# Two sets of small products of an RWKV-7 chunk solver issued together, one per quadrant of the array

## The chip, the cores and the metric

The kernel runs on one core of a Trainium2 chip. The metric is the device time of one execution in microseconds (us), as the median of several runs. TensorE is called PE here, VectorE DVE, ScalarE ACT, GpSimd POOL, and the queue on which most transfers are issued SP.

## The reference

One layer of a hybrid encoder block on a sequence of 512 positions with 1024 channels, all in float32. What matters here is branch B, the RWKV-7 recurrence with 8 heads of 64 channels:

```python
def step(state, inp):
    r_t, w_t, k_t, v_t, a_t, b_t = inp
    sa = jnp.einsum('bhvk,bhk->bhv', state, a_t)
    state = (state * w_t[:, :, None, :] + sa[..., None] * b_t[:, :, None, :]
             + v_t[..., None] * k_t[:, :, None, :])
    y = jnp.einsum('bhvk,bhk->bhv', state, r_t)
    return state, y
...
h = rmsnorm(x, attn_norm_g)
proj = h @ w_in
...
x = x + mixed @ w_out
...
x = x + (jax.nn.silu(u_gate) * u_val) @ w_ffn_down
```

Beside it stand branch A (stick-breaking attention, 8 heads, blocks of 128 queries), per-channel gates that merge the branches, and a feed-forward part with a depthwise convolution (2816 channels).

## The kernel before, in words

Channels lie on the 128 partitions and the 512 positions on the free axis. Dense products are float32 split into two rounded halves, and three products replace one (`mm1`, lines 131 to 136; the input projections by a loop of their own at line 864).

The first stage mixes three streams of work on PE until about 428 us: `dense_stream` (the columns of `w_in`, line 864, one weight tile after another, 24 products of 128x512 per tile), `att_stream` (attention), and four `rw_stream`, one for each pair of RWKV heads (pairs 0 to 3). Each stream is a generator: it issues a piece of work and yields the time that a planner, `interleave`, is to count for it on PE, and the time after which it may go on. The planner picks the next stream by these numbers alone (the table `LAT` and the constants in the yields), and dense products fill what the others leave. The program's own scheduler then orders each engine's instructions from there.

`rw_stream(p)` cuts the sequence into 8 chunks of 64 positions. For each chunk and head it builds the tile `QA` (products of keys, decays and queries, and the value columns 192 to 255), then inverts a triangular 64x64 matrix. The inverse goes in 32-row halves: the diagonal 32x32 blocks are solved on DVE (lines 531 to 541, buffers `N` and `U`), pass through memory (`su`, `st`, lines 544 to 546) and come back as `U1` (line 550) and `TT` (line 553). Then follow, per pair and in this order:

- `pa` (line 560): 16 products of 32x32, copied by DVE to `U1` (line 564);
- `pl` (line 571): 16 products of 64x64, the "Lak V" term, in two halves of four chunks, copied by ACT to `LV` (line 576);
- `pu` (line 582): 16 products of 32x32 that need `U1`, copied by DVE into the corner of `TT` (line 585);
- `px` (line 591): 16 products of 64x64, "T A", that need `TT`, scaled by DVE into `XA` (line 595);
- the serial chain over chunks (lines 607 to 633), whose first product needs `LV` and `TT`.

With `HROWS`, head 0 holds partitions 0 to 63 and head 1 64 to 127. `pl` reads the other head's partitions, so its two heads lie on one diagonal of the 128x128 array; `px` reads the head's own, so its two lie on the other diagonal. The psum tiles of `rw_stream` and of the small products of `att_stream` come from one pool of three banks (`rbank`).

SP issues, in one queue and in order, the weight loads (`wraw`, line 106), the stores and loads of the solver (lines 519 to 553). The weight tiles have two buffers; a tile is cast by ACT (line 108), and its remainder is made by ACT (line 121) and a POOL transfer (line 122).

Of the kernel before, what the change touches and what calls it, by code (L numbers as in the profile page):

```python
# [8 lines left out]
F32 = mybir.dt.float32  # L9
# [7 lines left out]
P = 128  # L17
# [9 lines left out]
CH = 64  # L27
NC = T // CH
# [24 lines left out]
def hybrid_block(ctx: ExitStack, tc: tile.TileContext, xT, w_in, vecs, decay_up, iclr_up, out_gate_up,  # L53
                 w_branch, w_out, w_up, w_down, out):
    nc = tc.nc
    V, A, G, PE = nc.vector, nc.scalar, nc.gpsimd, nc.tensor
# [127 lines left out]
    TT = cpool.tile([P, NC, CH], F32, name="TT")  # L184
# [15 lines left out]
    with tc.tile_pool(name="p0", bufs=1) as p0, \  # L200
# [76 lines left out]
        for j in range(2):  # L277
            hr = slice(64 * j, 64 * j + 64)
# [4 lines left out]
        for j in range(2):  # L283
            hr, ho = slice(64 * j, 64 * j + 64), slice(64 - 64 * j, 128 - 64 * j)
# [52 lines left out]
    rwp = ph1.enter_context(tc.tile_pool(name="rw", bufs=1, reuse_waits="tile"))  # L337
# [17 lines left out]
    def c3(a):  # L355
        return a.rearrange("p (c t) -> p c t", t=CH)

    def rbank():
        return bank(psr, "pr")

    HROWS = ((slice(0, 64), slice(64, 128)), (slice(64, 128), slice(0, 64)))
# [38 lines left out]
    def rw_stream(p):  # L400
# [7 lines left out]
        for j, bn in ((0, "db"), (1, "ib")):  # L408
            pl = rbank()
            PE.matmul(pl, lup[j][:, p * P : (p + 1) * P], wl2[j], start=True, stop=False)  # L410
            hr = slice(64 * j, 64 * j + 64)
# [54 lines left out]
        for h in range(2):  # L466
            hr = HROWS[h][0]
# [3 lines left out]
        for h in range(2):  # L471
            hr = HROWS[h][0]
# [18 lines left out]
        QAs = []  # L491
        for hf in range(2):
            QA = rwp.tile([P, 4, 2, 256], F32, tag="QA", name="QA", bufs=4)
            QAs.append(QA)
            for c2 in range(2):
                pp = [rbank(), rbank()]
                for j in range(2):
                    for h, (hr, _) in enumerate(HROWS):
                        ch = 4 * hf + 2 * c2 + j
# [3 lines left out]
                for j in range(2):  # L503
                    for h, (hr, _) in enumerate(HROWS):
                        ch = 4 * hf + 2 * c2 + j
                        PE.matmul(pp[h][:, j * P : (j + 1) * P], BK[hr, ch].rearrange("p s t -> p (s t)"),  # L506
                                  ARV[hr, ch, 0 : 2 + h : 1 + h], start=True, stop=True)
                for h in range(2):
                    V.tensor_tensor(QA[:, 2 * c2 : 2 * c2 + 2, h, 64:192],
                                    pp[h][:, 0:256].rearrange("p (j n) -> p j n", j=2),  # L510
                                    maskq[:, None, :].broadcast_to([P, 2, P]), op=ALU.mult)
                for h in range(2):
                    A.copy(QA[:, 2 * c2 : 2 * c2 + 2, h].rearrange("p j (s n) -> p j s n", s=4)[:, :, 0:4:3],
                           pp[h][:, 256:512].rearrange("p (j s n) -> p j s n", j=2, s=2))
# [42 lines left out]
        for ch in range(NC):  # L557
            for h in range(2):
                r0, r1 = slice(64 * h, 64 * h + 32), slice(64 * h + 32, 64 * h + 64)
                PE.matmul(pa[r1, ch * 32 : ch * 32 + 32], QAs[ch // 4][r0, ch % 4, h, 160:192], U1[r0, ch],  # L560
                          start=True, stop=True)
        for h in range(2):
            r1 = slice(64 * h + 32, 64 * h + 64)
            V.tensor_copy(U1[r1].rearrange("p q (k g) -> p q g k", g=4),
                          pa[r1, 0:256].rearrange("p (q g k) -> p q g k", q=NC, g=4))
        yield (430, 0)
        pl = rbank()
        for ch in range(NC):
            for h, (hr, ho) in enumerate(HROWS):
                QA = QAs[ch // 4]  # L570
                PE.matmul(pl[hr, ch * CH : (ch + 1) * CH], QA[ho, ch % 4, h, 128:192], QA[ho, ch % 4, h, 192:256],
                          start=True, stop=True)
            if ch == 3:
                yield (530, 0)
        LV = rwp.tile([P, NC, CH], F32, tag="LV", name="LV")
        A.copy(LV, c3(pl))
        yield (530, LAT["pl"][p])
        pu = rbank()
        for ch in range(NC):
            for h in range(2):  # L580
# [4 lines left out]
            V.tensor_copy(TT[r0, :, 32:64], pu[r0, 0:256].rearrange("p (q n) -> p q n", q=NC))  # L585
        yield (430, LAT["pu"][p])

        px = rbank()
        for ch in range(NC):
            for h, (hr, _) in enumerate(HROWS):  # L590
                PE.matmul(px[hr, ch * CH : (ch + 1) * CH], QAs[ch // 4][hr, ch % 4, h, 192:256], TT[hr, ch],
                          start=True, stop=True)
            if ch == 3:
                yield (530, 0)
        V.tensor_tensor(XA, c3(px), GC.broadcast_to([P, NC, CH]), op=ALU.mult)
        yield (530, LAT["x"][p])

        Rg = ARV[:, :, 0, :]
        G.tensor_tensor(Rg[:, 1:NC], Rg[:, 1:NC], GC[:, 1:NC].broadcast_to([P, NC - 1, CH]), op=ALU.mult)
# [3 lines left out]
        for ch in range(NC):  # L603
            QA, ci = QAs[ch // 4], ch % 4
# [12 lines left out]
            if ch < NC - 1:  # L617
                pS = rbank()
                for h in range(2):
                    PE.matmul(pS[64 * h : 64 * h + 64, 0:64], QA[:, ci, h, 0:64], QA[:, ci, h, 192:256],  # L620
                              start=True, stop=True)
# [8 lines left out]
            for h in range(2):  # L630
                PE.matmul(py[64 * h : 64 * h + 64, 0:64], QA[:, ci, h, 192:256], QA[:, ci, h, 64:128],
                          start=(ch == 0), stop=True, skip_group_check=True)
# [22 lines left out]
        cs = slice(p * P, (p + 1) * P)  # L655
# [160 lines left out]
    def dense_stream():  # L816
# [27 lines left out]
        while cur:  # L844
# [14 lines left out]
            else:  # L859
# [21 lines left out]
               x=(998, 814, 570, 793))  # L881
# [203 lines left out]
```

## Time and profile before

| | |
|---|---|
| median of 3 runs | 904.62 us (903.02 to 905.81) |
| the profiled execution | 903.5 us, of which the profiled span is 901.8 us |
| busy, share of the span | PE 96%, DVE 61%, ACT 57%, POOL 14% |
| TensorE clock granted, mean | 0.985 of full speed |
| transfers | 106.95 MB, mean 119 GB/s |

PE is busy nearly all the time, so time is read from what stands on PE, from the few stretches in which it stands still, and from those in which its clock is at half. A row of the trace gives start, duration, engine, line, operation, output and inputs, with a bracket for idle time just before and for what ended it. Matmuls overlap: how fast they follow each other is read from their starts, not their durations. A float32 product leaves two records, so 16 products are x32.

### The profile page before, as it was taken

The numbers are of one execution on the slowest core, as the hardware profiler recorded it, in microseconds if no ns is written. First come the engines' busy times: TensorE is split into PE (matmuls) and PEld (weight loads), VectorE is DVE, ScalarE is ACT, GpSimd is POOL, SyncE is SP. The second block draws the span as 40 slices with busy tenths as digits, with TensorE's granted clock in tenths as the row PEclk, the third lists the DMA queues.
The fourth block names the chain that finished last, engine by engine and source line by source line (L and its number), as shares of the span: only waits on it lengthen the run. The fifth ranks groups of instructions, "written<-read, shape, count | busy, mean of one in ns | idle before, by whom it ended". The sixth has DMA issues, their size and how long they took to land.

```text
span 901.8 us, 12963 instructions
## 1 busy us (share of the span) xinstructions
PE 864.2 (96%) x4718; PEld 668.9 (74%) x4718; DVE 553.9 (61%) x1115; ACT 513.6 (57%) x909; POOL 129.7 (14%) x200
## 2 busy tenths in 40 slices
PE   5898889999999998899999999999999999999998
PEld 3566656676767776667887878888888888888886
DVE  7566797685785583345565557777777777522222
ACT  7887879866876784778554445444444444321120
POOL 2332433224322431222000000000000000000000
PEclk9798999999999999999999999999999999999999
DMA  7365646756548536843764443333333333243431
GB/s 211 84 140 108 134 93 131 150 119 128 120 89 171 124 87 123 180 101 82 240 190 135 140 117 94 93 94 96 103 104 95 94 94 94 88 129 100 128 100 41
DMA packets 175136, 106.95 MB, mean 119 GB/s; under 512 B 29568, under 2 KB 156672, under 8 KB 175072
## 3 DMA queue, kind: packets, MB, share of 16 engines
q1 hardware_dynamic: 161392, 81.61, 32.6%
q0 software_dynamic: 10656, 19.40, 12.7%
q10 hardware_dynamic: 3024, 5.11, 1.7%
q8 instruction: 37, 0.61, 0.3%
q14 instruction: 27, 0.22, 0.1%
HBM read 78.31 MB, written 8.39 MB: 96 GB/s over the span
## 4 chain that ended last, share of the span: by engine, by line
PE 77%; ACT 6%; DVE 6%; DMA 5%; issue 4%; POOL 1%; SPq 1%; ACTq 0%; POOLq 0%; DVEq 0%
PE pf L136 17%; PE pf L135 17%; PE pf L134 17%; PE pd L864 14%; DMA wraw<-in_w_in 3%; DVE tm L537 1%; ACT wlo L121 1%; DVE U L539 1%; PE pz L747 1%; PE pr L506 1%; PE pr L620 1%; PE pr L607 1%; ACT whi L108 1%; ACT t L69 1%; DMA su<-U 1%
## 5 line engine op out<-in xcount | busy, mean ns | idle before, releaser
L108 ACT CAST whi<-wraw 128x1024 fp32r<-128x1024 f32 (+1 forms) x132 | 130.0, 985 | 180.1 <-PE pf L135 143.3
L124 DVE TENSOR_TENSOR wlo<-wraw,whi 128x512 fp32r<-128x512 f32 (+1 forms) x178 | 114.5, 680 | 82.1 <-ACT whi L108 77.7
L134 PE MATMUL pf<-h2h,whi 128*128 128x512 f32 x352 | 137.3, 390 | 0.0
L135 PE MATMUL pf<-h2l,whi 128*128 128x512 f32 x352 | 136.9, 389 | 0.0
L136 PE MATMUL pf<-h2h,wlo 128*128 128x512 f32 x352 | 136.9, 389 | 0.0
L864 PE MATMUL pd<-hhi,whi 128*128 128x512 f32 x296 | 122.7, 414 | 3.3 <-ACT gs L802 2.6
L864 PE MATMUL pd<-hlo,whi 128*128 128x512 f32 x296 | 121.8, 411 | 0.0
L122 POOL DMA_DIRECT2D wlo<-wraw x74 | 65.3, 918 | 193.1 <-ACT wlo L121 118.0
L864 PE MATMUL pd<-hhi,wlo 128*128 128x512 f32 x296 | 85.2, 409 | 2.0 <-DMA wlo<-wraw 1.9
L135 PEld LDWEIGHTS pf<-h2l,whi 128*128 128x128 f32 x352 | 66.1, 188 | 14.0 <-issue 0.2
L134 PEld LDWEIGHTS pf<-h2h,whi 128*128 128x128 f32 x352 | 66.1, 188 | 13.9 <-issue 0.2
L136 PEld LDWEIGHTS pf<-h2h,wlo 128*128 128x128 f32 x352 | 66.1, 188 | 13.6
L864 PEld LDWEIGHTS pd<-hhi,whi 128*128 128x128 f32 x296 | 57.1, 193 | 16.8 <-ACT gs L802 3.0
L136 PE MATMUL pf<-dh,wlo 128*128 128x512 f32 x176 | 69.3, 394 | 0.0
L134 PE MATMUL pf<-dh,whi 128*128 128x512 f32 x176 | 69.3, 394 | 0.0
L135 PE MATMUL pf<-dl,whi 128*128 128x512 f32 x176 | 69.3, 394 | 0.0
L864 PEld LDWEIGHTS pd<-hhi,wlo 128*128 128x128 f32 x296 | 53.8, 190 | 16.3 <-DMA wlo<-wraw 5.0
L864 PEld LDWEIGHTS pd<-hlo,whi 128*128 128x128 f32 x296 | 57.0, 192 | 12.0 <-issue 0.7
L1024 DVE TENSOR_TENSOR u<-pf,rs 128x512 f32<-128x512 f32 x44 | 30.3, 688 | 38.7 <-PE pf L136 38.6
L128 ACT CAST dh<-cv 128x512 fp32r<-128x512 f32 x22 | 13.7, 621 | 62.0 <-DVE cv L1033 62.0
L121 ACT ACTIVATE wlo<-whi 128x512 fp32r<-128x512 f32 x74 | 45.5, 629 | 2.4 <-ACT QA L615 0.7
L135 PEld LDWEIGHTS pf<-dl,whi 128*128 128x128 f32 x176 | 32.9, 187 | 8.3
(308 smaller groups left out, 1626.5 us busy)
## 6 DMA issues: line engine op xcount, KB each, us to landing
wraw<-in_w_up SPq DMA_DIRECT2D x44, 512.0 KB, 3.8
wraw<-in_w_in SPq DMA_DIRECT2D x41, 512.0 KB, 4.0
wlo<-wraw POOLq DMA_DIRECT2D x74, 256.0 KB, 3.8
wraw<-in_w_down SPq DMA_DIRECT2D x16, 512.0 KB, 4.1
wraw<-in_w_branch SPq DMA_DIRECT2D x16, 256.0 KB, 3.1
wraw<-in_w_out SPq DMA_DIRECT2D x8, 512.0 KB, 4.1
gd<-gs ACTq DMA_DIRECT2D x13, 256.0 KB, 3.6
g<-gd SPq DMA_DIRECT2D x13, 256.0 KB, 2.8
```

The costliest lines, as they stand in the source:

```text
L69: ins = A.activation(o, i, func, **kw)
L108: after(A.copy(hi[:, 0:nk], raw[:, 0:nk]), state["last"])
L121: A.mul(lo[:, 0:n], f(hi[:, k0 : k0 + n]), -1.0)
L122: G.dma_start(lo[:, 0:n], raw[:, k0 : k0 + n], accum_op=ALU.add)
L124: V.tensor_tensor(lo[:, 0:n], raw[:, k0 : k0 + n], f(hi[:, k0 : k0 + n]), op=ALU.subtract)
L128: A.copy(hi, src)
L134: PE.matmul(ps, hi, ah, start=first, stop=False)
L135: PE.matmul(ps, hi, al, start=False, stop=False)
L136: PE.matmul(ps, lo, ah, start=False, stop=last)
L506: PE.matmul(pp[h][:, j * P : (j + 1) * P], BK[hr, ch].rearrange("p s t -> p (s t)"), ARV[hr, ch, 0 : 2 + h : 1 + h], start=True, stop=True)
L864: PE.matmul(ps, w_, a, start=(n == 0), stop=(n == len(todo) - 1))
L1024: V.tensor_tensor(u, ps, rs2, op=ALU.mult)
```

## The change

`pl` is no longer issued between `pa` and `pu`, but after `pu`, chunk by chunk with `px`: for each chunk the four products (two heads of each) go out in a row, and each lies in its own quadrant of the array. Both psum banks are taken at once. The planner now counts 650 + 650 for the joint block where it counted 530 four times, and what was the delay after `pl` is the delay between `pa` and `pu`. The copy to `LV` comes after the joint block.

```diff
-        yield (430, 0)
-        pl = rbank()
-        for ch in range(NC):
-            for h, (hr, ho) in enumerate(HROWS):
-                QA = QAs[ch // 4]
-                PE.matmul(pl[hr, ch * CH : (ch + 1) * CH], QA[ho, ch % 4, h, 128:192], QA[ho, ch % 4, h, 192:256],
-                          start=True, stop=True)
-            if ch == 3:
-                yield (530, 0)
-        LV = rwp.tile([P, NC, CH], F32, tag="LV", name="LV")
-        A.copy(LV, c3(pl))
-        yield (530, LAT["pl"][p])
+        yield (430, LAT["pl"][p])
         pu = rbank()
...
         yield (430, LAT["pu"][p])
 
-        px = rbank()
+
+        pl, px = rbank(), rbank()
         for ch in range(NC):
-            for h, (hr, _) in enumerate(HROWS):
-                PE.matmul(px[hr, ch * CH : (ch + 1) * CH], QAs[ch // 4][hr, ch % 4, h, 192:256], TT[hr, ch],
-                          start=True, stop=True)
+            QA, cs = QAs[ch // 4][:, ch % 4], slice(ch * CH, (ch + 1) * CH)
+            for h, (hr, ho) in enumerate(HROWS):
+                PE.matmul(pl[hr, cs], QA[ho, h, 128:192], QA[ho, h, 192:256], start=True, stop=True)
+                PE.matmul(px[hr, cs], QA[hr, h, 192:256], TT[hr, ch], start=True, stop=True)
             if ch == 3:
-                yield (530, 0)
+                yield (650, 0)
+        LV = rwp.tile([P, NC, CH], F32, tag="LV", name="LV")
+        A.copy(LV, c3(pl))
         V.tensor_tensor(XA, c3(px), GC.broadcast_to([P, NC, CH]), op=ALU.mult)
-        yield (530, LAT["x"][p])
+        yield (650, LAT["x"][p])
```

Since the planner's numbers changed, it places other work differently too, from pair 0 on. In the changed program `pu` is line 571, `pl` line 582, `px` line 583, the `LV` copy line 587, and later lines stand 7 lower (dense products line 857, masks and values 737 to 757).

**Pair 1 on PE and ACT.** `pr` are the pool's three banks, `pz` and `po` those of attention. PE before, from `pa` on:

```order
L560 MATMUL pr<-U_95,QA 32x32 x16
L864 MATMUL pd<-hhi,whi 128x512
L864 MATMUL pd<-hlo,whi 128x512
L864 MATMUL pd<-hhi,whi 128x512
L571 MATMUL pr<-QA 64x64 x8
L714 MATMUL pz<-q_1714,k_1830 128x384
L715 MATMUL pz<-q_1714,klo_91 128x384
L716 LDWEIGHTS idb
L716 MATMUL pz<-mskb,idb 128x128
L571 MATMUL pr<-QA 64x64 x8
```

PE in the changed program, at the start of the joint block:

```order
L737 MATMUL pz<-ach,none 128x256
L737 MATMUL pz<-acl,none 128x256
L740 MATMUL pz<-sph_2294,ntri 128x384
L740 MATMUL pz<-spl_2295,ntri 128x384
L756 MATMUL po<-wth,vt 128x256
L757 MATMUL po<-wtl,vt 128x256
L582 MATMUL pr<-QA 64x64
L583 MATMUL pr<-TT,QA 64x64
L582 MATMUL pr<-QA 64x64
L583 MATMUL pr<-TT,QA 64x64
```

ACT before, around the copy to `LV`:

```order
L121 ACTIVATE wlo<-whi 128x512
L69 ACTIVATE e<-pz 128x384
L576 COPY LV<-pr 128x512
L69 ACTIVATE e<-e 128x384
L69 ACTIVATE wth<-pz 128x256
```

ACT in the changed program:

```order
L69 ACTIVATE e<-pz 128x512
L69 ACTIVATE e<-e 128x512
L69 ACTIVATE wth<-pz 128x384
L69 ACTIVATE e<-e 128x512
L69 ACTIVATE w<-pz 128x384
L128 CAST sph_2557<-e 128x512
L587 COPY LV<-pr 128x512
```

The two sets of products alternate one by one, 16 times, in pairs 1 to 3 (in pair 3 two products of attention stand between the halves). In pair 0 the scheduler issues 15 of `pl` in a row, then 15 of `px`, then the last of each. The `LV` copy of pair 1 moved behind the six ACT steps of a 512-wide score tile.

**Pair 1 on SP**, from the solver's store to the loads of the next stage. Before:

```order
L546 DMA st<-N 512x1x8 x4
L553 DMA TT<-su 32x8x32 x3
L519 DMA sc<-QA 32x4x32 x4
L550 DMA U_95<-st 32x8x32 x2
L553 DMA TT<-su 32x8x32
L106 DMA wraw<-in_w_in 128x8x128
```

In the changed program:

```order
L546 DMA st<-N 512x1x8 x4
L553 DMA TT<-su 32x8x32 x3
L550 DMA U_95<-st 32x8x32 x2
L553 DMA TT<-su 32x8x32
L106 DMA wraw<-in_w_in 128x8x128
L519 DMA sc<-QA 32x4x32 x8
```

The loads of `U1` no longer stand behind four stores of pair 2's `QA`.

**Pair 3 on SP**, the same place. Before:

```order
L546 DMA st<-N 512x1x8 x4
L106 DMA wraw<-in_w_in 128x8x128
L553 DMA TT<-su 32x8x32
L550 DMA U_95<-st 32x8x32
L553 DMA TT<-su 32x8x32
```

In the changed program:

```order
L546 DMA st<-N 512x1x8 x4
L553 DMA TT<-su 32x8x32 x3
L550 DMA U_95<-st 32x8x32
L106 DMA wraw<-in_w_in 128x8x128
L550 DMA U_95<-st 32x8x32
```

A weight load of the dense stream now stands behind the first load of `U1`, which waits for the solver's stores to land.

## Rows read from the trace of the kernel before

**Rows 1.** The page: busy time and share of each engine, and the clock by slices.

```profile
PE 864.2 (96%) x4718; PEld 668.9 (74%) x4718; DVE 553.9 (61%) x1115; ACT 513.6 (57%) x909; POOL 129.7 (14%) x200
...
PEclk9798999999999999999999999999999999999999
```

**Rows 2.** Waits of PE from 58 to 430 us: us in total, times, longest.

```profile
PE pd L864 <- ACT gs L802: 2.6, 1, 2.6
```

**Rows 3.** Timeline of PE, pair 0: start, duration, engine, line, operands, shapes.

```profile
156.65 1.15 PE L571 MATMUL pr<-QA 64*64 64x64 f32 x32
157.73 0.69 PE L582 MATMUL pr<-TT,U 32*32 32x32 f32 x32
...
159.71 1.15 PE L591 MATMUL pr<-TT,QA 64*64 64x64 f32 x32
```

**Rows 4.** Timeline of PE, two places where two tiles of the array are used.

```profile
144.38 0.23 PE L501 MATMUL pr<-ident,ARV 64*128 64x64 f32 x2
144.45 0.23 PE L501 MATMUL pr<-ident,BK 64*128 64x64 f32 x2
...
167.83 0.34 PE L620 MATMUL pr<-QA 128*64 128x64 f32 x4
168.00 0.29 PE L631 MATMUL pr<-QA 128*64 128x64 f32 x4
```

**Rows 5.** Timeline of PE, pair 1: the start of `pa`.

```profile
218.54 0.21 PE L560 MATMUL pr<-U,QA 32*32 32x32 f32 x2 [1.81 <-DMA U<-st]
219.06 0.62 PE L560 MATMUL pr<-U,QA 32*32 32x32 f32 x27 [0.31 <-DMA U<-st]
```

**Rows 6.** Timeline of SP's queue, pair 1.

```profile
214.61 1.87 SPq L519 DMA_DIRECT2D sc<-QA  x4
216.53 0.92 SPq L550 DMA_DIRECT2D U<-st  x2
```

**Rows 7.** Chain that ended last, pair 1: start, us, what.

```profile
220.84 1.05 PE pr L571 x16
...
229.12 1.38 PE pd L864 x6
230.50 0.61 PE pr L591 x16
```

**Rows 8.** Windows view: length; PE, PEld, DVE, ACT, POOL busy; PEclk; DMA share; GB/s.

```profile
220.00:224.00 4.00, 4.00 (x39) 2.81 (x38) 2.13 (x5) 0.52 (x2) 1.89 (x4) 0.57 0.76 206
```

**Rows 9.** Timelines of PE, ACT and DVE, pair 1, and the `LV` copy's line.

```profile
228.01 0.23 PE L716 MATMUL pz<-mskb,idb 128*128 128x128 bf16 x1
...
228.28 0.60 ACT L69 ACTIVATE e<-pz 128x512 f32<-128x512 f32 x1 [0.92 <-PE pz L716]
...
231.65 0.63 ACT L128 CAST sph<-e 128x512 fp32r<-128x512 f32 x1
...
230.47 0.69 DVE L721 SCALAR_TENSOR_TENSOR e<-pz,e 128x512 f32<-128x512 f32 x1 [1.59 <-ACT e L69]
...
L576 ACT COPY LV<-pr x4: 581/586/587, 157.8 to 376.5; 128x512 f32<-128x512 f32 x4
```

**Rows 10.** Timeline of SP's queue, pair 3.

```profile
345.40 9.23 SPq L546 DMA_DIRECT2D st<-N  x4
354.80 0.50 SPq L106 DMA_DIRECT2D wraw<-in_w_in  x1
...
357.28 0.33 SPq L550 DMA_DIRECT2D U<-st  x1
```

**Rows 11.** Timeline of DVE, pair 3.

```profile
370.34 1.26 DVE L564 COPY U<-pr 32x256 f32<-32x256 f32 x2 [2.63 <-PE pr L560]
376.16 0.69 DVE L674 TENSOR_TENSOR wtl<-sq,wth 128x512 fp32r<-128x512 f32 x1 [4.55 <-ACT sq L69]
376.77 0.75 DVE L680 SCALAR_TENSOR_TENSOR rawq<-rawq,qg,sq 128x512 f32<-128x512 f32 x1
...
379.63 0.87 DVE L585 COPY TT<-pr 32x256 f32<-32x256 f32 x2
```

## The prediction

> **What bounds the kernel now.** I read the page first. PE is busy for 864.2 of 901.8 us, 96%, DVE for 61% and ACT for 57% [rows 1]: TensorE's queue sets the time, and only three things can change it: work on PE, stretches in which PE stands still, and its clock. The slices of the clock show digits below 9 near the start and, later, hardly at all [rows 1]. The change touches the first stage alone, until about 428 us; the rest is dense products that follow unchanged, so a microsecond that PE gains there arrives at the end. Next I read the waits of PE in that stage and the timelines around the four places where `pa`, `pl`, `pu`, `px` stand. PE waits twice for the loads of `U1` at pair 1's `pa`, 1.81 and 0.31 us [rows 5], and once 2.6 us for the evacuation of a dense bank, late in the stage [rows 2]. Outside those, the moved products run without a gap.
>
> **The joint block.** Sixteen products of `pl` hold PE from 156.65 to 157.73, 1.08 us, and sixteen of `px` start a row of the same length [rows 3]. Both already run two heads at a time. What the trace lacks is four 64x64 tiles at once. Its parts are there. Two row halves that share all columns: each row of two transposes follows the last after 0.07 us though it lasts 0.23, so two go out every 0.07 [rows 4]. Two column halves that share all 128 rows: four records of line 620 are followed by the next group after 0.17 us [rows 4], which one at a time, at the 0.07 of the transposes, would need 0.28. Bounds: if four run at once, the joint block costs 1.08 in place of 2.16 us, a gain of 1.08 per pair; if two, the gain is 0. A loss I exclude, since the block issues the same products in the same tile size. I take 1.08, because each half of the mechanism is seen. In pair 0 the products don't alternate, and I count nothing. For pair 3 see below. Pairs 1 and 2: **-2.2 us**.
>
> A rule speaks against this. The Trainium skill, "TensorE: Matmul & The Clock Gate", Part 3 on row and column tiling, says that a weight load overlaps running matmuls only when its row group differs. `pl` of one head and `px` of the other share their row group, so by that rule only two would run at once and the term would be 0. The rows of line 620 [rows 4] speak against it, but for two tiles, not four. It is a rival below.
>
> **Pair 1's wait.** The loads of `U1` were issued at 216.53, behind four stores (line 519) that held SP's queue from 214.61 for 1.87 us [rows 6]. In the new order they stand ahead of those stores, so they go out about 1.9 us sooner. `pa` also comes later on PE: the new order has 8 more dense products between pair 0's `pa` and pair 1's, at 1.38 / 6 = 0.23 us each [rows 7] 1.8 us, and 8 transposes fewer, at 0.07 [rows 4] 0.6 us. 1.9 + 1.8 - 0.6 is more than the 1.81 + 0.31 = 2.12 us of the wait [rows 5]. The bounds are 0 and -2.1; I take **-2.1 us**. Those dense products are only moved: they are missing later, where something else must cover.
>
> **The clock behind that wait.** After it, half of `pl` took 1.05 us, where half of `px` at full clock took 0.61 [rows 7]. From 220 to 224 us the granted clock averaged 0.57 [rows 8], which is mostly the lower of its two levels, 1.2 GHz against 2.4. PE had stood still before it fell. At full clock the same work needs 4.0 x 0.57 = 2.3 us, so 1.7 is lost. Without the wait there is nothing to lower the clock there; another wait could do so elsewhere. Bounds 0 and -1.7; I take **-1.7 us**.
>
> **Cover that goes.** (a) `pl` stood between `pa` and `pu` while DVE copied `U1`, two copies in 1.26 us [rows 11]. In the new order pair 0 still has its 9 dense products and 8 transposes there, pair 1 has 8 transposes and nine wide products, pair 2 six dense products (1.4 us) and 8 transposes, pair 3 nine (2.1 us): 0. (b) `pl` ran long before `px`, so `LV` was ready early. Now the copy starts after the joint block, and the chain's first product waits for it. In pair 1 the copy stands behind the ACT steps of a 512-wide score. Before, that score ended at 228.24 [rows 9]; DVE's step of it ended at 231.16, the cast `sph` could follow at 231.2 without the weight cast that stood ahead of it, for 0.63 us, and the copy takes 0.59 [rows 9]: 232.4, that is 4.2 us after the score. PE has in that time six mask and value products (0.9 us, an estimate from six of them at 0.15), the joint block (1.1), three dense products (0.7), a small score and tile changes (0.5): 3.2. The chain waits **+1.0 us**; bounds 0 (the copy comes in time) and 2. In pair 2 it stands behind four casts of the keys, and no row times that line; between 0 and pair 1's 1.0 I take **+0.5 us**. In pairs 0 and 3 four or six full-width dense products stand between block and chain, about 0.9 to 1.4 us against 0.6 for the copy: 0.
>
> **Pair 3.** `px` needs DVE's copies into `TT`. In the new order DVE does them behind a split (`wtl`, at 376.16) and the scaling of `q` (376.77 to 377.52) [rows 11], which wait for ACT and not for PE. With the copies' 0.87 us `px` can't start before 378.4; before, the copies ended at 380.5 [rows 11]. PE has three dense products fewer between `pa` and `px`, and no `pl`, so it arrives early and waits there. The saving of this pair is spent on that wait: **0**, between -1.1 (arriving in time) and +1.
>
> **Pair 3's weight load.** Before, it was issued at 354.80, right behind the solver's stores, and the first `U1` load at 357.28, once the stores had landed [rows 10]. Now it stands behind that load: it starts at 357.7 or so unless the solver is done sooner. This tile was already the one PE waited for, 2.6 us [rows 2]. Bounds 0 and +2.9; the solver's last DVE step now stands ahead of three other steps that shared its end, which brings the stores forward, so I take the lower third, **+1.0 us**.
>
> **Sum:** -2.2 - 2.1 - 1.7 + 1.0 + 0.5 + 0 + 1.0 = -3.5 us against the profiled execution's 903.5, so 900.0. The median, 904.62, lies 1.1 above that execution: **901.1 us**. A measurement of this kernel can tell about 0.3%, 2.7 us, from no change.
>
> **Rivals.**
>
> 1. *Two at a time.* The four quadrants don't run at once (the rule above, or the queue not looking far enough ahead). The rest stays: -3.5 + 2.2 = -1.3, 903.3 us. For: no row shows four. Against: both halves of it [rows 4].
> 2. *The weight tile starves PE (slower).* Pair 3's load waits for the solver's stores. If the solver ends 3 us later than before against the dense stream, the load starts at 360.7, 5.9 us later than 354.80 [rows 10], PE stands still that much longer, and the clock falls behind it (+1.7, as in rows 8). -3.5 - 1.0 + 5.9 + 1.7 = +3.1, 907.7 us. It decides from a load that starts some 2.8 us late with the fall of the clock, 4.5 without. For: the load's new place and the wait it already causes [rows 2]. Against: the U1 loads get out of the way of the next tile.
> 3. *The time isn't on the path.* Each pair's chain meets the same landings, casts and copies as before, PE only waits for them elsewhere: 904.6 us. For: pair 3 shows just that. Against: the waits of PE in the middle of the stage are few.
> 4. *Nothing new waits.* -2.2 - 1.1 - 2.1 - 1.7 = -7.1, 897.5 us. Against: the new places of the `LV` copy.
>
> **How the numbers follow.** Forecast 0.42, with a range of its own of 899 to 903; rival 1 0.15; rival 2 0.15; rival 3 0.18; rival 4 0.10. Faster by over 0.3% (below 901.9): nearly all of the forecast (0.38), rival 4, a little of rival 1 (0.02): 0.50. Slower by over 0.3% (above 907.3): 0.13 of rival 2 and 0.04 of rival 3: 0.17. Within: 0.33. The range goes from rival 4's 897.5 to 907.0, which leaves out most of rival 2 and little else.
>
> **What would show it.** In the profile after: records of the joint block in pairs 1 to 3 in groups of four starts and some 1.1 us for all 32 products (right), or 2.1 (rival 1); `pa` of pair 1 without a wait for `U1`, and the clock at 1.00 from 215 to 230 us; the chain's first product waiting for `LV` by about a microsecond in pair 1; the wait for the dense bank after 355 us at 2.6 to 5.5 us. The prediction is wrong if PE's idle time in the stage grows by more than the block saves, above all if the clock falls behind a new wait.

## The result, and the profile after

The changed kernel took 909.46 us (median of 17 runs, 904.49 to 913.80), the kernel before 904.06 in the same comparison: a ratio of 1.0052 (95% interval 1.0035 to 1.0068). It is 0.5% slower, where 901.1 us was forecast and 907.0 was the range's upper end. The profiled execution took 909.66 us (span 908.0, mean granted clock 0.979), 6.2 us more than that of before.

The page of the changed kernel, the same lines as [rows 1]:

```profile
PE 866.8 (95%) x4718; PEld 669.4 (74%) x4718; DVE 554.2 (61%) x1115; ACT 513.5 (57%) x909; POOL 133.1 (15%) x200
...
PEclk9799999999998899999999999999999999999999
```

The work of each engine is what it was. New is the clock: the slices from 272 to 318 us show an 8 where they showed a 9. PE's waits from 58 to 430 us, the view of [rows 2] (us in total, times, longest):

```profile
PE pr L501 <- ACT QA L513: 5.4, 3, 3.1
...
PE pd L857 <- DMA wlo<-wraw: 3.6, 4, 1.3
PE pr L583 <- DVE TT L574: 2.8, 1, 2.8
...
PE pr L600 <- ACT LV L587: 1.0, 1, 1.0
```

The wait for `U1` in pair 1 [rows 5] is gone from the head of the list. The longest is now 3.1 us at line 501, a place whose waits the prediction never mentions: the first products that build `QA` for the next pair. Pair 1 first, PE's timeline from `pa` to the end of the joint block:

```profile
216.53 0.69 PE L560 MATMUL pr<-U,QA 32*32 32x32 f32 x32
...
223.30 0.27 PE L582 MATMUL pr<-QA 64*64 64x64 f32 x1
223.30 0.27 PE L583 MATMUL pr<-TT,QA 64*64 64x64 f32 x1
223.31 0.27 PE L582 MATMUL pr<-QA 64*64 64x64 f32 x1
223.32 0.27 PE L583 MATMUL pr<-TT,QA 64*64 64x64 f32 x1
223.41 0.22 PE L582 MATMUL pr<-QA 64*64 64x64 f32 x1
...
224.39 0.50 PE L857 MATMUL pd<-hlo,whi 128*128 128x512 f32 x1
...
226.72 0.33 PE L600 MATMUL pr<-LV,TT 64*64 64x64 f32 x4 [1.03 <-ACT LV L587]
```

`pa` runs in one piece with no wait. Four products, one per quadrant, start within 20 ns, and all 32 products hold PE from 223.30 to 224.39, 1.09 us, as long as 16 of them before [rows 3]. The clock is at 1.00 from 220 to 224. Then the chain waits 1.03 us for `LV`. So far the sizes are as forecast. Now the place of the 3.1 us, first PE's timeline:

```profile
280.62 0.28 PE L501 MATMUL pr<-ident,BK 64*128 64x64 f32 x2
...
283.30 0.96 PE L857 MATMUL pd<-hhi,wlo 128*128 128x512 f32 x3
287.36 0.36 PE L501 MATMUL pr<-ident,BK 64*128 64x64 f32 x1 [3.10 <-ACT QA L513]
```

And ACT's at the same time:

```profile
281.34 1.26 ACT L679 CAST q<-rawq 64x512 fp32r<-64x512 f32 x2 [0.82 <-DVE rawq L673]
285.99 1.04 ACT L108 CAST whi<-wraw 128x1024 fp32r<-128x1024 f32 x1 [3.40 <-DMA wraw<-in_w_in]
286.94 0.64 ACT L513 COPY QA<-pr 128x256 f32<-128x256 f32 x2
```

PE needs a bank of `rbank`'s three. ACT would free it with the copy of line 513, whose input is ready (in the run below that takes the cast away, the same copies start at 284.02), but on ACT a weight cast stands ahead of the copy, and the cast waits 3.40 us for its load. Behind the wait, the windows of the changed kernel (columns as in [rows 8]):

```profile
284.00:288.00 4.00, 0.90 (x7) 0.64 (x6) 0.51 (x2) 2.01 (x4) 0.00 (x0) 0.79 0.74 188
288.00:292.00 4.00, 4.00 (x54) 3.49 (x53) 2.30 (x5) 0.75 (x3) 0.96 (x2) 0.50 0.46 75
292.00:296.00 4.00, 4.00 (x40) 2.90 (x39) 0.97 (x4) 1.76 (x4) 2.19 (x5) 0.50 0.00 0
296.00:300.00 4.00, 4.00 (x20) 3.01 (x21) 2.11 (x5) 1.89 (x4) 1.03 (x2) 0.50 0.41 71
300.00:304.00 4.00, 4.00 (x71) 2.96 (x70) 2.65 (x6) 2.75 (x6) 2.53 (x5) 0.58 0.61 146
304.00:308.00 4.00, 4.00 (x32) 2.96 (x31) 1.77 (x5) 2.73 (x7) 0.10 (x1) 1.00 0.43 131
```

The clock goes to the lower level and stays there until about 303. From 284 to 304 its mean is 0.57, where before it was 1.00: 20 x 0.43 = 8.6 us. About 0.5 us of that lie in the wait itself, while PE stood still, so some 8 are lost behind it. With the wait that is 11 us, more than the change could have saved.

In the kernel before the same cast stood directly ahead of the same copies in ACT's queue. Its timeline of ACT at that place:

```profile
290.49 1.05 ACT L108 CAST whi<-wraw 128x1024 fp32r<-128x1024 f32 x1 [0.30 <-PE pd L864]
291.44 0.64 ACT L513 COPY QA<-pr 128x256 f32<-128x256 f32 x2
```

And where PE begins to build pair 3:

```profile
284.77 0.69 PE L560 MATMUL pr<-U,QA 32*32 32x32 f32 x32
285.39 0.68 PE L571 MATMUL pr<-QA 64*64 64x64 f32 x16
...
286.80 0.68 PE L571 MATMUL pr<-QA 64*64 64x64 f32 x16
...
288.30 0.27 PE L501 MATMUL pr<-ident,BK 64*128 64x64 f32 x1
```

There the build of pair 3 began at 288.30, and the cast waited for PE (0.30 us) and not for its load. In the changed kernel the build begins at 280.62, 7.7 us sooner, but the cast only 4.5 us sooner (285.99 for 290.49). Pair 1's chain is done 5.3 us sooner (its last copy to `Y` starts at 259.9, before at 265.2). The other 2.4 us come from PE's order around the build: before, `pa` and `pl` of pair 2 stood ahead of it (the rows above); in the changed kernel `pl` is gone from there and `pa` comes at 288.94, behind the stall. PE gained time in both ways and ran into a weight tile that had not gained as much.

### The profile page after: what moved, and what is told of

It reads as the page before. It is cut to its first block, busy times and chain, and to the rows that moved or that the text cites. A ratio compares the mean times of both kernels' runs of the same rounds, so it can differ in the third digit from the quotient of the medians.

```text
span 908.0 us, 12964 instructions
## 1 busy us (share of the span) xinstructions
PE 866.8 (95%) x4718; PEld 669.4 (74%) x4718; DVE 554.2 (61%) x1115; ACT 513.5 (57%) x909; POOL 133.1 (15%) x200
## 4 chain that ended last, share of the span: by engine, by line
PE 75%; DVE 8%; ACT 6%; DMA 5%; issue 4%; SPq 1%; POOL 0%; ACTq 0%; POOLq 0%; DVEq 0%
PE pf L136 17%; PE pf L134 17%; PE pf L135 17%; PE pd L857 13%; DMA wraw<-in_w_in 4%; DVE tm L537 2%; DVE U L539 2%; ACT wlo L121 1%; PE pr L613 1%; PE pz L740 1%; ACT whi L108 1%; PE pr L600 1%; SPq L546 1%; PE pr L506 1%; ACT t L69 1%
## 5 line engine op out<-in xcount | busy, mean ns | idle before, releaser
L134 PEld LDWEIGHTS pf<-dh,whi 128*128 128x128 f32 x176 | 32.9, 187 | 8.2
```

What stands on the lines that cost most here:

```text
L134: PE.matmul(ps, hi, ah, start=first, stop=False)
```

## The experiments

"Build" is the longest wait of PE at line 501 for pair 3, "clock" the mean from 284 to 304 us, both of each run's profiled execution. Where a star stands, the wait ends with another step of ACT (`sq`), which also frees a bank. Ratios are against the kernel before on the same chip.

| kernel | median, us | ratio (95%) | build, us | clock |
|---|---|---|---|---|
| changed, again | 910.33 | 1.0059 (1.0037 to 1.0080) | 3.5 | 0.57 |
| U twice | 910.27 | 1.0064 (1.0042 to 1.0086) | 3.9 | 0.83 |
| block apart | 909.20 | 1.0045 (1.0028 to 1.0061) | 2.0* | 0.74 |
| cast on POOL | 907.81 | 1.0029 (1.0015 to 1.0044) | 2.8 | 0.66 |
| solver first | 911.93 | 1.0066 (1.0046 to 1.0085) | 3.2* | 0.66 |
| both | 912.03 | 1.0075 (1.0060 to 1.0089) | 3.5* | 0.74 |
| planner 1060 | 910.15 | 1.0058 (1.0039 to 1.0077) | 2.8* | 0.50 |
| tile on POOL | 898.74 | 0.9938 (0.9915 to 0.9962) | none | 1.00 |
| tile on POOL, apart | 910.92 | 1.0041 (1.0018 to 1.0065) | 1.9* | 0.52 |
| three raw buffers | 893.97 | 0.9879 (0.9858 to 0.9900) | none | 1.00 |
| three raw buffers, again | 893.04 | 0.9865 (0.9846 to 0.9883) | none | 1.00 |
| three raw buffers, apart | 894.58 | 0.9881 (0.9863 to 0.9899) | 1.0 | 0.67 |
| before, U twice | 903.75 | 0.9979 (0.9966 to 0.9992) | 0.2 | 1.00 |
| before, tile on POOL | 903.63 | 0.9987 (0.9973 to 1.0001) | 0.4 | 1.00 |
| before, three raw buffers | 893.34 | 0.9871 (0.9849 to 0.9893) | none | 1.00 |
| before, three raw buffers, again | 892.79 | 0.9865 (0.9850 to 0.9880) | none | 1.00 |

**One execution?** The changed kernel, profiled once more.

> The changed kernel itself, profiled once more and timed. Its first profile shows PE standing still for 3.10 us at 284.26 (for ACT's copies of QA, which stand behind a weight cast) and the clock at the lower level from 286.33 to 303.39. Theory 'held queue' (a memset that waits for the solver's store holds the weight stream back, so PE stalls and the clock falls): the stall is in the order of the program, so it shows again, between 2.5 and 3.7 us, and the clock falls behind it; 907 to 912 us. Rival 'bad draw' (that profile was one unlucky execution): the stall or the low stretch is missing, and the time is 904 to 907.

The wait is there again, 3.49 us, and the clock is 0.57. It belongs to the order, not to one execution (the fastest of the 17 timed executions, 904.49 us at a mean clock of 0.990, may have lost less; it has no trace).

**What makes the load late.** It went out at 279.81; the two transfers of remainders that free its buffer had left POOL at 274.56, behind a memset of `U` that waits for the solver's store.

```diff
-    U = rwp.tile([P, 8, 32], F32, name="U")
+    U_two = [rwp.tile([P, 8, 32], F32, name=f"U{i}") for i in range(2)]
...
-        G.memset(U, 0.0)
+        U = U_two[p % 2]; G.memset(U, 0.0)
```

> The changed kernel with two buffers for U, so that POOL's memset of the next pair's U does not wait for the store of this pair's. PE's and ACT's orders stay as they are. Theory 'held queue': the two weight remainders that left POOL at 274.56 go out by about 271 and 273, the load at 279.81 starts about 2.5 us sooner, the wait of 3.10 us shrinks below 0.8, and the clock doesn't fall there, which returns 2.5 + 8 us: 898 to 902 us. Rival 'short of cover' (with pl gone from between pa and pu the dense stream runs ahead of its loads, whatever POOL does): the wait stays above 2 us and the time at 907 to 911.

The first transfer went out right behind ACT's step (275.59, with ACT's done at 275.29; in the changed kernel 274.56 and 270.83), so the memset had held them. (This profile runs late throughout: the cast of the tile before stands at 279.81 in place of 275.24.) The wait stayed, 3.9 us: the load now stood on SP behind the solver's stores and loads and went out at 286.43. One link was removed and another, on SP, took over, so the memset alone is not the cause.

The same edit on the kernel before:

> The kernel before with two buffers for U: the control for the run above. In its trace two remainders of the same pair stand behind the same memset too (268.34 and 269.99), but PE shows only 0.42 us of waiting near them. Theory 'held queue': the wait is covered there, so within 0.3% of the kernel before, 902 to 906. Rival 'U alone' (the second buffer is a gain by itself, with or without the joint block): faster by as much as in the changed kernel, 895 to 899.

A ratio of 0.9979: about 2 us, with nothing at the build to remove.

**The block itself.** Taken apart in the same place:

```diff
-        for ch in range(NC):
+        for half, s in ((0, 0), (0, 1), (1, 0), (1, 1)):
+            for ch in range(4 * half, 4 * half + 4):
...
-                PE.matmul(pl[hr, cs], QA[ho, h, 128:192], QA[ho, h, 192:256], start=True, stop=True)
-                PE.matmul(px[hr, cs], QA[hr, h, 192:256], TT[hr, ch], start=True, stop=True)
+                for hr, ho in HROWS:
+                    PE.matmul((pl, px)[s][hr, cs], QA[(ho, hr)[s], HROWS.index((hr, ho)), (128, 192)[s] : (192, 256)[s]],
+                              QA[ho, HROWS.index((hr, ho)), 192:256] if s == 0 else TT[hr, ch], start=True, stop=True)
...
```

> The changed kernel with the joint block taken apart: eight products of pl, then eight of px, twice, in the same place and with the planner's numbers unchanged. No four quadrants at once: the block takes 2.2 to 2.6 us in place of 1.16 in pair 1. The program's scheduler also moves one weight load on SP, pair 2's, from ahead of four solver stores to behind them. Theory 'held queue': what slows the changed kernel isn't the block, so it is slower than the changed kernel by what the quadrants save, 1 to 3 us, or by more where that load lands later still: 910 to 915. Rival 'the block itself' (four at once disturb what follows): faster than the changed kernel, 903 to 907.

As slow as the joined one (1.0045 against 1.0059, intervals that overlap). The edit undoes only part of the concurrency: the block took 1.56 us in pair 1, not the 2.2 to 2.6 expected, and PE still waits 2.0 us at the build. So nothing speaks for four at once as what costs, but this run by itself doesn't exclude it; the run with the tile on POOL, below, does.

**The solver, and ACT.** In the changed kernel the solver of pair 2 ends at 268.9 in place of 262.3, since its last steps alternate on DVE with pair 3's preparation. That could be why PE is left with dense products alone. A rival: the late cast on ACT is enough. The first edit moves that one cast to POOL (it is the 27th of the dense stream); nothing else changes place:

```diff
-        after(A.copy(hi[:, 0:nk], raw[:, 0:nk]), state["last"])
+        state["n"] = state.get("n", -1) + 1; (G.tensor_copy if state["n"] == 26 else lambda o, i: after(A.copy(o, i), state["last"]))(hi[:, 0:nk], raw[:, 0:nk])
```

> The changed kernel with one weight cast, the one that ACT did at 285.99 ahead of four copies of QA, moved to POOL; nothing else changes place on any engine. Theory 'blocked ACT' (PE's 3.10 us at 284.26 come from the copies of QA that stand on ACT behind a cast whose load is late): the copies run at about 284.6, the wait shrinks below 1 us, and the stretch of low clock behind it goes or gets short: 909.8 - 2.5 - (4 to 8) = 899 to 903 us. Rival 'tile late anyway' (PE has drawn the dense stream so far ahead that without this tile it has nothing to do): PE does the build and the 32-row products a little sooner and then stands still at the next dense product for as long, the clock falls all the same, 908 to 911 us.

ACT's timeline with the cast on POOL:

```profile
284.02 0.70 ACT L513 COPY QA<-pr 128x256 f32<-128x256 f32 x2 [1.29 <-DVE QA L509]
287.90 0.63 ACT L121 ACTIVATE wlo<-whi 128x512 fp32r<-128x512 f32 x1 [3.18 <-POOL whi L108]
288.44 0.63 ACT L513 COPY QA<-pr 128x256 f32<-128x256 f32 x2
```

And PE's:

```profile
285.34 0.69 PE L560 MATMUL pr<-U,QA 32*32 32x32 f32 x32
288.85 0.36 PE L501 MATMUL pr<-ident,BK 64*128 64x64 f32 x1 [2.82 <-ACT QA L513]
```

Two copies now run at 284.02, and PE goes on to `pa`. Then ACT stands again, for the remainder of the same tile, with the next two copies behind it. The block moved by one step. The ratio is 1.0029 where the changed kernel had 1.0052 and 1.0059, with intervals that overlap, so it is open how much came back.

The second edit puts pair 3's preparation and pair 1's last steps behind the solver's last step by order-only dependences on DVE (`behind` adds one; two of the four places are shown):

```diff
-        V.tensor_copy(ut, U.rearrange("p k t -> p t k"))
+        state["sol", p] = V.tensor_copy(ut, U.rearrange("p k t -> p t k"))
...
-        V.scalar_tensor_tensor(kk, k, vcol("keyk", p), kk, op0=ALU.mult, op1=ALU.mult)
+        behind(V.scalar_tensor_tensor(kk, k, vcol("keyk", p), kk, op0=ALU.mult, op1=ALU.mult), p == 3)
...
```

> The changed kernel with pair 3's preparation on DVE (from the scaling of kk on, and two projections) and pair 1's last steps put behind the last step of pair 2's solver, with which they alternate in the changed kernel from 258 to 268.5; PE's order stays. Theory 'late solver' (this alternation makes the solver end at 268.9 where it ended at 262.3 before; meanwhile PE runs through its dense products and out of weights): the solver ends by 263, pa of pair 2 starts 3 to 6 us sooner than 288.9, no wait of PE over 1 us from 275 to 295, no stretch of low clock there: 898 to 903 us. Rival 'tile late anyway': the weight loads, which move on SP too, are late still, a wait of 2 us or more and a low clock stay: 907 to 911 us.

The timeline of DVE, the solver's last step:

```profile
262.80 0.41 DVE L541 COPY N<-U 128x256 f32<-128x256 f32 x1
```

ACT's timeline:

```profile
281.57 1.05 ACT L108 CAST whi<-wraw 128x1024 fp32r<-128x1024 f32 x1 [3.89 <-DMA wraw<-in_w_in]
```

PE's waits from 275 to 300 us:

```profile
PE pr L501 <- ACT sq L69: 3.2, 1, 3.2
```

The solver ends at 263.2 (262.3 in the kernel before), and nothing is gained. The solver's transfers now stand ahead of the weight loads on SP, the cast of the tile before the late one waits 3.89 us on ACT, and what stands behind it is a step of the attention (`sq`) that holds another of the three banks. So an early solver is not enough. Whether the late one has a part in the stall stays open, since the edit made another tile late.

> Both edits together: the cast on POOL and the solver first. 'Late solver' and 'blocked ACT' name two links of one chain, so together they return no more than the better of the two, 898 to 903 us. If they are separate costs, the sum of both gains. Under 'tile late anyway' 907 to 911.

No gain either, for the same reason: the tile that is late is now the one before, and its cast is still on ACT (3.80 us of waiting, at 280.95).

**The tile off ACT altogether.** Cast and both remainders of the 27th tile on POOL:

```diff
+        (G.tensor_copy if state["n"] == 26 else lambda o, i: after(A.copy(o, i), state["last"]))(hi[:, 0:nk], raw[:, 0:nk])
...
+        if state.get("n") == 26:
+            G.tensor_tensor(lo[:, 0:n], raw[:, k0 : k0 + n], f(hi[:, k0 : k0 + n]), op=ALU.subtract)
+        elif state.get("dma"):
```

> The changed kernel with all the work on one weight tile, the late one (its cast, and both remainders), on POOL, so that ACT does nothing for it. With the cast alone on POOL, the wait of 3.10 us came 1.7 us later (2.82 us at 286.03), since the next two copies of QA still stood on ACT behind the first remainder of the same tile. Theory 'blocked ACT': now no copy of QA stands behind that tile, PE goes through pair 3's build and meets the tile at its next dense product, by then cast: waits of PE from 280 to 295 under 1 us together, no stretch of low clock or a short one, 900 to 904 us. Rival 'tile late anyway': the wait of about 3 us moves on to the dense product of that tile, and the clock falls: 907 to 910 us.

The timeline of ACT:

```profile
284.07 1.03 ACT L513 COPY QA<-pr 128x256 f32<-128x256 f32 x3 [1.29 <-DVE QA L509]
```

POOL's:

```profile
286.65 1.04 POOL L107 CAST whi<-wraw 128x1024 fp32r<-128x1024 f32 x1 [7.42 <-DMA wraw<-in_w_in]
```

PE's:

```profile
285.39 0.69 PE L560 MATMUL pr<-U,QA 32*32 32x32 f32 x32
286.01 0.27 PE L501 MATMUL pr<-ident,BK 64*128 64x64 f32 x1
```

And the window from 284 to 304 us:

```profile
284.00:304.00 20.00, 19.10 (x244) 13.76 (x244) 12.63 (x29) 13.25 (x33) 9.13 (x13) 1.00 0.41 102
```

The tile is as late as ever (its cast starts at 286.65, where it was 285.99), but only POOL waits for it. PE goes through the build, and when it comes to the tile's products the tile is there. No wait, clock 1.00, and some 10 us less than the changed kernel (0.9938 against 1.0052; the medians, from two comparisons, differ by 10.7). The joint block is in place here, so it is not what costs. This shows the cause: not the late tile alone, but ACT's queue behind the tile.

The control is the same edit on the kernel before:

> The kernel before with the same weight tile's work moved from ACT to POOL; nothing else changes place. The control for the run on the changed kernel that went to 898.7 us. There the tile's load was late against PE; before, its cast at 290.49 has no wait for a load behind it and PE waits 0.42 us near it. Theory 'blocked ACT' (the edit repairs a stall that only the changed order has): within 2 us of the kernel before, 903 to 907, so that the changed kernel with the edit is 0.5 to 0.8% faster than this one. Rival 'a gain of its own' (work taken off ACT helps either way): 897 to 901 us.

0.9987: the edit alone gives nothing that can be told from no change. So it repairs what the change broke, and the change without that stall is worth 0.9938 / 0.9987 = 0.995, some 4.4 us (an estimate across two comparisons).

**The planner's numbers.**

```diff
-                yield (650, 0)
+                yield (1060, 0)
...
-        yield (650, LAT["x"][p])
+        yield (1060, LAT["x"][p])
```

> The changed kernel with the planner counting 1060 + 1060 for the joint block, as much as it counted for pl and px before (4 x 530), in place of 650 + 650. Theory 'planner' (what slows the changed kernel is that the planner, counting 820 less for each pair, places dense work and pair 3's preparation otherwise): the order comes close to the one before, the wait at pair 3's build is under 1 us, 898 to 903 us. Rival 'the move' (pl behind pu is enough to upset pair 2, whatever is counted): a wait of 2 us or more and a low clock there, 907 to 911 us.

The wait (2.8 us) and the low clock (0.50) are there, with a cast at 279.93 that waits 4.95 us on ACT. Counting as much as before doesn't take the stall away: the build still begins ahead of pair 2's `pa` (281.19 and 287.46). That `pl` behind `pu` decides it is the likelier reading, but the order differs from that of before in more than this.

**A third raw buffer.** One of three places that allocate the tile; the other two get the same:

```diff
-        raw = wpool.tile([P, KT, P], F32, tag="wraw", name="wraw")
+        raw = wpool.tile([P, KT, P], F32, tag="wraw", name="wraw", bufs=3)
```

> The changed kernel with three buffers for the raw weight tile in place of two, so that a load needn't wait until both remainders of the tile before last are done (the load at 279.81 went out when the transfer issued at 275.37 had landed). The scheduler moves some other work with it. Theory 'two buffers' (the weight stream can't run further ahead than two tiles, so PE, which now has nothing but dense products from 260 to 281, outruns it): the loads that were at 269.8 and 279.8 go out 3 to 8 us sooner, no wait over 1 us at pair 3's build, no stretch of low clock there: 897 to 903 us. Rival 'blocked queues' (it is the order on SP and ACT, not the buffers): the load stands behind the solver's transfers on SP all the same, 907 to 911.

> The kernel before with three raw buffers, the control for the run above. Theory 'two buffers': before, PE meets no late tile in pair 2, and gains at most its 2.58 us of waiting at 358.86 and a little more: 900 to 904 us. If the third buffer is a gain of its own, 5 us or more here too, 896 to 900.

Both are faster than the kernel before by some 12 us, more than any theory said, and equal to each other. Most of it is waiting, and not at the build alone: by the pages PE stands still for 901.8 - 864.2 = 37.6 us in the kernel before, which waits only 0.42 us at the build, and for 891.4 - 863.1 = 28.3 us in the same kernel with three buffers. No weight cast on ACT waits for a load any more from 262 to 296 us. These are the fastest versions of the study. Timed again together:

> The changed kernel with three raw weight buffers, timed once more beside the two runs below. Theory 'freed' (with the weight stream repaired the change gives what its block saves, 3.3 us less what waits take its place): 1 to 3 us faster than the kernel before with three buffers. Rival 'nothing left' (what the change repairs in pair 1, the wait for U1 and the clock behind it, the third buffer repairs too, and the block's gain goes into the waits for LV, for the remainders and for the bank): within 1 us of it, as the first runs showed (893.97 and 893.34).

> The kernel before with three raw weight buffers, once more, as the other half of that comparison: 892 to 895 us by both.

893.04 and 892.79, both at 0.9865 (0.9846 to 0.9883 and 0.9850 to 0.9880). With the weight stream repaired the change is worth nothing that shows. Its block does run four at a time (1.16 us in pairs 1 and 2 from the first start to the last end), but PE waits for other things. PE's waits from 140 to 430 us, first of the changed kernel with three buffers:

```profile
PE pr L560 <- DMA U<-st: 2.5, 2, 2.3
PE pd L857 <- DMA wlo<-wraw: 2.1, 2, 1.3
PE pr L600 <- ACT LV L587: 1.0, 1, 1.0
PE pr L692 <- ACT QA L513: 0.9, 1, 0.9
```

Then of the kernel before with three buffers:

```profile
PE pr L560 <- DMA U<-st: 2.5, 1, 2.5
PE pd L864 <- ACT rawq L374: 1.1, 1, 1.1
```

With the joint block PE waits 1.0 us for `LV`, 0.9 for a bank and 2.1 for remainders, without it 1.1 for a dense bank, and pair 1's wait for `U1`, the largest thing the change removed, is gone in both but for 0.2 us (the 2.3 and 2.5 us of line 560 are pair 0's). In the two profiles PE is busy 861.2 us with the joint block and 863.1 without, and stands still 29.8 us and 28.3. So most of what the block saves is waited away; these are single executions, and that the waits listed are the whole reason is argued, not shown.

**Four quadrants alone.** Two attempts to price them by taking the block apart where nothing stalls:

> The changed kernel with that tile on POOL and with the joint block taken apart (eight products of pl, then eight of px, twice, in the same place). Against the 898.7 us with the block joined it shows what the four quadrants give once no stall covers it. Theory 'quadrants': 1.08 us in each of pairs 1 to 3, less where the block is waited for anyway: 901 to 903 us. Rival 'hidden': 898 to 900. The scheduler moves one load on SP as it did with the first kernel of this kind, so a wait of over 1 us at pair 3's build in its trace would make it undecided.

Undecided by its own condition: it waits 1.9 us at the build, behind the cast of another tile (4.79 us on ACT), and its clock is 0.52. Two of its twelve executions took 903.12 and 903.90 us, at mean clocks of 0.988 and 0.985; the other ten took 907.4 to 912.9, at 0.974 to 0.981.

> The changed kernel with three raw buffers and the joint block taken apart, eight products of pl, then eight of px, twice, in the same place. With two buffers this comparison was undecided, since a late tile stopped PE. If PE has no wait over 1 us for a late tile from 260 to 300 us, it shows what four quadrants at once give. Theory 'quadrants': 1.08 us in each of pairs 1 to 3, 2 to 4 us slower than with the block joined. Rival 'hidden': within 1 us of it.

894.58 against 893.04 us, ratios 0.9881 (0.9863 to 0.9899) and 0.9865: slower by 1.5 us with intervals that overlap, so not settled. In pair 1 the block took 1.57 us from its first start to its last end, not 2.2: eight of one set run into eight of the other, so taking it apart that way undoes only part of the concurrency. And the 1.5 us can't be put down to the block: PE waits 1.24 us for `U1` in pair 1 and 0.99 at the build, and its clock falls behind that wait (profiled was the slowest of the five executions, 896.95 us). With the block joined PE waits 0.2 us for `U1`, not at all at the build, and the clock is 1.00. PE's timeline with the block apart, and the windows behind it:

```profile
282.31 0.27 PE L501 MATMUL pr<-ident,BK 64*128 64x64 f32 x1 [0.99 <-ACT QA L513]
```

```profile
282.00:290.00 8.00, 7.69 (x95) 6.18 (x96) 3.30 (x8) 3.46 (x9) 3.19 (x6) 0.60 0.66 148
290.00:298.00 8.00, 8.00 (x89) 6.02 (x89) 4.56 (x9) 4.64 (x9) 3.56 (x6) 0.54 0.52 110
```

## Why the prediction was wrong

**Joint block, -2.2: right in size.** 32 products in 1.09 us in pair 1; in pair 2 they fell into the low clock (301.92 to 303.66, 1.74 us) and ran at full speed once the stall was gone. The rule of the Trainium skill, "TensorE: Matmul & The Clock Gate", Part 3, which by the prediction's reading would have let only two run at once, is not borne out: `pl` and `px` that share their rows start within 20 ns. Rival 1 falls.

**Pair 1's wait, -2.1, and the clock behind it, -1.7: right.** `pa` runs without a wait, and the clock is 1.00 from 220 to 224. Of the two reasons given for the wait one is seen: the loads of `U1` go out at 213.95, 2.6 us sooner than before, which is enough by itself. That PE would come later to `pa` is not seen: it is there at 216.53, and before at 216.73 (218.54 less the wait).

**`LV`, +1.0 and +0.5.** 1.03 us in pair 1, none in pair 2.

**Pair 3.** As forecast, `px` waits for `TT`, 2.82 us, where `pu` had waited 1.34: 1.5 us more. The 0 counted on a saving of the block that this wait would spend, and that isn't there either: the two halves run at a clock that falls behind the wait (a mean of 0.61 from 381 to 385 us) and take 1.0 and 1.1 us. The weight load went out at 354.00, not later than before (354.80), and PE waits for remainders there (1.24 + 0.40 + 1.31 = 2.95 us) as long as it had waited for the bank [rows 2] and one remainder (2.58 + 0.35): 0 in place of +1.0. Rival 2, as placed, did not happen.

**What failed** is the step "Cover that goes". The prediction says under "Pair 1's wait" that the moved dense products "are missing later, where something else must cover", and this step then looks only at the readers of `pl`, `pu` and `px`. It puts what else the moved products had covered at nothing, without a reason. The place that was hurt was the next pair's build, where PE arrives 7.7 us sooner and needs a bank that ACT frees. I had compared what moved in the queues; on ACT the cast stood ahead of those copies before as well, and only the times had shifted against each other, but on PE a part of the build had come ahead of pair 2's `pa`, and the prediction doesn't ask what the build waits for there. Rival 2 named the mechanism (a late weight tile stops PE, the clock falls behind it) for pair 3 and for SP's queue; it came in pair 2 and through ACT's. That its time, 907.7 us, lies near the measured one is luck: it added 5.9 us of waiting and 1.7 of clock, and measured were 3.1 and 8.0. Rival 3, that the time isn't on the path, is what the two kernels with three buffers look like, but not these two. The prediction's own sign of being wrong came true: PE's idle time grew by 3.6 us (37.6 to 41.2 over the span), more than the block saves, and the clock fell behind a new wait.

**The price** failed too. "Another wait could do so elsewhere" was bounded at 1.7 us, the one case seen; it was about 8.

The account between the two profiled executions: +3.1 - 0.4 for the build, +8.0 for the clock behind it, -2.1 and -1.7 in pair 1, -1.1 for the block there, -0.7 for the block of pair 2 (four halves of 0.61 us before, 1.74 now), +1.0 for `LV`, +1.5 in pair 3, which makes +7.6; measured are +6.2. Another 1.7 us lie ahead of all four places in the sequence: from 58 to 100 us the mean clock was 0.92 before and 0.96 in the changed kernel. In the second profile of the changed kernel it was 0.88 there, so that comes with the execution and not with the change. With it the account makes +5.9. Without the stall the kernel is 0.62% faster than before (0.38 to 0.85%), 5.6 us, and 4.4 against its control; the forecast sum was 3.5.

## What to carry to other kernels

When an edit brings the busiest engine forward, nothing has to move in the other queues for one of them to hold it up: follow each buffer that it will need next to the instruction that frees it, and look for what stands ahead of that on its engine and waits for a load. A conversion of a streamed tile in one queue with the copies that free the busiest engine's banks is a risk as soon as the stream has no slack; where the tile came in time (the control), moving it gave nothing. Here a third raw buffer for the stream gave 1.2 to 1.4%, more than the edit under study. And a wait on TensorE is to be priced with the clock behind it, with a wide upper bound.

## What the runs showed of the hardware

Four 64x64 products that lie in four quadrants of the array, issued in turn, ran at once: 32 took 1.09 us, as long as 16 in two quadrants.

The low clock lasted much longer than the wait ahead of it, and not by the wait's length. Behind 3.10 us at the build the mean was 0.50 from 288 to 300 us, although PE was busy all that time (the windows in the first section). Behind 3.94 us with `U` twice it was 0.56 and 0.59 from 292 to 300 us and 1.00 from 300 on, and behind 0.99 us with three buffers and the block apart it was low for some 16 us (the rows above). With the tile on POOL and the block apart, 1.9 us of waiting were followed by a mean of 0.52 from 284 to 304 us:

```profile
284.00:304.00 20.00, 19.80 (x132) 14.29 (x131) 10.18 (x22) 7.58 (x16) 7.68 (x10) 0.52 0.42 100
```

Yet behind the 2.82 us in pair 3 the changed kernel's clock was nearly whole again 4 us later:

```profile
381.00:385.00 4.00, 3.97 (x66) 2.90 (x66) 2.25 (x5) 3.91 (x6) 0.86 (x1) 0.61 0.48 108
385.00:389.00 4.00, 4.00 (x21) 2.71 (x20) 1.94 (x4) 3.35 (x7) 0.86 (x1) 0.96 0.72 154
```

What tells these cases apart was not tried. The spread goes with the clock too: the 17 runs of the changed kernel go from 904.49 us at a mean clock of 0.990 to 913.80 at 0.977, and 0.013 of 908 us is 11.8 us, which more than covers the 9.3 between them.
